# A two-layer transformer trunk on one core: the first key block's value product made 512 queries wide, and the second layer's x turned four blocks earlier

## The chip, the cores and the metric

One core of one Trainium2 chip runs the whole program. The metric is device time in microseconds (us). The kernel before takes 1125.02 us, the median of three runs (1124.52 to 1125.22). One further execution was profiled; every duration below is from that one.

## The reference, cut to what matters

```python
for l in range(2):
    h = rmsnorm(x, attn_norm[l])
    sb_q, sb_k, sb_v, df_q, df_k, df_v = split(h @ w_in[l])          # 1024 -> 6 x 512
    sb_out = stick_breaking_attention(sb_q, sb_k, sb_v)              # 8 heads of 64, weights w, out = w @ v
    df_heads = differential_attention(rope(df_q), rope(df_k), df_v)  # 4 heads, two softmaxes, (p0 - lam*p1) @ v
    df_out = rmsnorm(df_heads, subln_norm[l]) * (1 - lambda_init)
    x = x + concat([sb_out, df_out]) @ w_o[l]
    h = rmsnorm(x, mlp_norm[l])
    x = x + square(relu(h @ w_ff1[l])) @ w_ff2[l]                    # 1024 -> 4096 -> 1024
out = rmsnorm(x, final_norm)
```

There are 512 positions. Query and key blocks are 128 long, and all attention is causal: query block i looks at key blocks 0 to i. Everything is float32.

## The kernel before, in words

**Arithmetic.** A float32 operand is split into a rounded half (`hi`, made by ScalarE) and the rest (`lo`, subtracted on VectorE). A product is three matmuls, hi x hi, hi x lo, lo x hi (`three`, L295), or two where the values are kept as one tile of both halves (the stick-breaking heads, L655 and L656). Weights come from HBM as 512 KB tiles and are split on the chip (`split_part`, L116 on ScalarE and L132 on VectorE), two or four units ahead of TensorE.

**Order of the work.** x lies turned, features on partitions and positions along the free axis. In a layer, TensorE runs a dense stream (input projections `p...`, then the output projection `wo`) and the attention is woven into it: `dense` (L777) yields after every few matmuls, `attn` (L734) is a generator that is advanced as a planner's credit allows (L821 to L846). Attention goes in units: kind (`d` differential, `s` stick-breaking), head block b, m, and half. A unit with half 0 holds query blocks 0 and 1, one with half 1 holds query blocks 2 and 3. A unit passes through three stages, one iteration of L737 apart:

- `s1_df`, `s1_sb` (L547, L569): scores into a PSUM bank of tag `s` (three banks), then the weights on ScalarE, VectorE and GpSimd. Each has two or more score steps.
- `s2` (L621), two iterations later (`LAG2`): transposes of the weights into banks of tag `t` (two of them), then a split into `xh`, `xl` (key blocks 0 and 1) and `zh`, `zl` (key blocks 2 and 3). A half-0 unit writes columns 0 to 383 of `xh` and `xl`: key block 0 for query blocks 0 and 1 in columns 0 to 255, then key block 1 for query block 1. A half-1 unit writes columns 384 to 895, where 640 to 895 are key block 0 for query blocks 2 and 3.
- `s3` (L640), three iterations later (`LAG3`): weights times values into the one bank of tag `o`. The table in L648 to L650 says which columns go where: a half-0 unit multiplies key block 0 for 256 queries, the half-1 unit key block 0 for the other 256, then key block 1 for 384 and key blocks 2 and 3 for 256 each. After that the head's result is read out (L671, L672; L674 splits the last one into `vdh`, `vdl`, which the second half of the output projection reads).

`behind_scores` (L716) sets what follows the score steps of an iteration: for a half-1 unit key blocks 0 and 1, then `s2` of another unit, then key blocks 2 and 3; for a half-0 unit `s2`, then key block 0. `attn` takes one step of this after each score step.

**The dense block behind attention.** The first quarter of the hidden units (group 0) goes in eight blocks f of 24 matmuls each, k = 0 to 7 (L1203). Behind each block stand its evictions (`evict_whole`, L960) and one piece of `h_form` (L998): sums and differences of blocks of h, which the later three groups multiply, seven products instead of eight (`quad_group`, L1034; `FORMS`). Then come the products with the second matrix, in the order `FORMS2` = 11, x3, 21, x2, x1, x4, 22 (L1215), accumulated in chains named X, V, Y, W. Their weights lie in `kept` tiles (names q00 to q20, and the tile `waves` for the sixth). `fetch` (L866) issues the load on SyncE's queue; for form x3 a second load on GpSimd's queue adds another quadrant on top.

**Where the layers differ.** The first layer parks x in HBM and makes the differences of h in x itself. The second layer keeps x, since `forth` (L1113) has to transpose it into the tiles y behind blocks 4 to 7 (L1209 to L1211); its differences are made in three of the `kept` tiles (L981, L982), so the loads into these come late: x3 behind block 6 and 21 behind block 7 (L1019), where the first layer has them behind blocks 3 and 5.

Of the kernel before, what the change touches and what calls it, by code (L numbers as in the profile page):

```python
# [17 lines left out]
P = 128  # L18
# [146 lines left out]
def trunk(ctx, tc, opened, xT, w, w2, w1, gfin, lamv, cos, sin, out):  # L165
# [169 lines left out]
    for l in range(L):  # L335
        with ExitStack() as actx:
# [7 lines left out]
            vd_hi = ap_.tile([P, 4, 512], F32R, tag="vdh", name=f"vdh{l}")  # L344
            vd_lo = ap_.tile([P, 4, 512], F32R, tag="vdl", name=f"vdl{l}")
            ms_hi, ms_lo = vd_hi, vd_lo
            xh, xl = (ap_.tile([P, 896], F32R, tag=f"x{n}", name=f"x{n}{l}") for n in "hl")
            zh, zl = (ap_.tile([P, 512], F32R, tag=f"z{n}", name=f"z{n}{l}") for n in "hl")
            nc.gpsimd.memset(zh[:, 0:128].bitcast(F32), 0.0)
            nc.gpsimd.memset(zl[:, 0:128].bitcast(F32), 0.0)  # L350

            def tt(name):
                return a2.tile([P, S], F32, tag="t", name=name, bufs=TB)
# [284 lines left out]
                yield (0.77 if half else 0.33) + (also() if also else 0.0)  # L638

            def s3(u, parts_):  # L640
                half, b, m, kind = u["half"], u["b"], u["m"], u["kind"]
                key = (kind, b, m)
                if half == 0:
                    heads[key] = bank("o", f"O{l}{kind}{b}{m}")
                k = 2 if kind == "s" else 3
                cost = 0.0
                for kb in parts_:
                    t, at_, to, w = {  # L648
                        (0, 0): ((xh, xl), 0, 0, 256), (1, 0): ((xh, xl), 640, 256, 256), (1, 1): ((xh, xl), 256, 128, 384),
                        (1, 2): ((zh, zl), 256, 256, 256), (1, 3): ((zh, zl), 0, 256, 256)}[(half, kb)]  # L650
                    o = heads[key][:, to : to + w]
                    wh, wl = (e[:, at_ : at_ + w] for e in t)
                    if kind == "s":
                        v = vs[:, kb, 2 * b + m, :]
                        nc.tensor.matmul(o, v, wh, start=(half == 0), stop=False)  # L655
                        nc.tensor.matmul(o, v, wl, start=False, stop=(kb == 3))  # L656
                    else:
                        three(o, (vd_hi[:, kb, b * P : (b + 1) * P], vd_lo[:, kb, b * P : (b + 1) * P]), (wh, wl),
                              half == 0, kb == 3)
                    cost += w * k * MMC  # L660
                if half == 1 and parts_[-1] != 3:
                    yield cost
                    return
                if half == 1:
                    o = heads.pop(key)
                    if kind == "s":
                        if m == 0:
                            heads[("mt", b)] = a2.tile([P, S], F32, tag="mt", name=f"mt{l}{b}", bufs=MTB)
                        mt = heads[("mt", b)]
                        oc = tt(f"oc{l}{b}{m}")[0:64, :]  # L670
                        nc.scalar.copy(oc, o[64:128, :])  # L671
                        nc.vector.tensor_add(mt[64 * m : 64 * m + 64, :], o[0:64, :], oc)  # L672
                        if m == 1:
                            split(ms_hi[:, b, :], ms_lo[:, b, :], mt)  # L674
                    else:
                        os_ = a2.tile([P, S], F32, tag="mt", name=f"os{l}{b}", bufs=MTB)
                        sqo = tt(f"sqo{l}{b}")
                        nc.scalar.activation(sqo, o, AF.Square)
                        nc.scalar.activation(os_, o, AF.Copy, scale=gsub[:, l : l + 1])
                        rc = a3.tile([P, 4], F32, tag="rc", name=f"rc{l}{b}")  # L680
                        late.append((b, os_, sqo, rc))
                yield cost

            units = []
# [43 lines left out]

            def values(u, parts_):
                while not ok(("v" + u["kind"], u["b"])):  # L730
# [119 lines left out]
        with ExitStack() as fctx:  # L850
# [126 lines left out]
                split(hi[:, 6, :], lo[:, 6, :], F[:, 3, :])  # L977

            early, late_ = slice(0, 256), slice(256, 512)
            if last:  # L980
                ta, tb_, tc_ = (kept[k].rearrange("p (a t) -> p a t", a=4) for k in ((1, 0), (1, 1), (2, 0)))  # L981
                td, te = ta, tb_  # L982
            else:
# [14 lines left out]
            def h_form(k):  # L998
                if k == 1:
                    for c in range(4):  # L1000
                        a = nc.scalar.activation(ta[:, c, :], x[:, c, early], AF.Copy, scale=gcol("mlp", l, c))
                        behind(a, ends["h"][0])
                    if last:
                        scaled(tb_, 0, late_, ta, ALU.subtract)
                elif k == 2:
                    scaled(tc_, 4, early, ta, ALU.subtract)
                    if not last:
                        scaled(tb_, 0, late_, ta, ALU.subtract)
                    split(*h_forms["x3"], tb_)
# [9 lines left out]
                for form, at in (("x3", 6 if last else 3), ("21", 7 if last else 5)):  # L1019
                    if k == at:  # L1020
                        for c in range(GP // 2):
                            fetch(0, form, c)

            def temp(k, name):
                if k == 3:
# [353 lines left out]
```

## Time and profile before

| | |
|---|---|
| median of three runs | 1125.02 us |
| the profiled execution: time, span from first to last instruction | 1125.43 us, 1123.7 us |
| TensorE matmul, busy | 1115.3 us (99%) |
| VectorE, ScalarE, GpSimd, busy | 905.5, 683.8, 155.7 us |
| mean granted TensorE clock | 0.999 |
| matmuls | 6421 |

A profile row of a group gives the source line, engine, operation, names (out<-in), shapes and count; a timeline row begins with the start from the span's beginning and the duration, and ends with the idle time before it and who ended it. PE is TensorE's matmul side, PEld its weight loads, DVE is VectorE, ACT ScalarE, POOL GpSimd, SP SyncE; an engine's name with q is its instruction queue. Matmuls are pipelined: the duration of one is longer than the distance between two starts, and only the distance says what one costs.

### The profile page before, as it was taken

The numbers are of one execution on the slowest core, as the hardware profiler recorded it, in microseconds if no ns is written. First come the engines' busy times: TensorE is split into PE (matmuls) and PEld (weight loads), VectorE is DVE, ScalarE is ACT, GpSimd is POOL, SyncE is SP. The second block draws the span as 40 slices with busy tenths as digits, with TensorE's granted clock in tenths as the row PEclk, the third lists the DMA queues.
The fourth block names the chain that finished last, engine by engine and source line by source line (L and its number), as shares of the span: only waits on it lengthen the run. The fifth ranks groups of instructions, "written<-read, shape, count | busy, mean of one in ns | idle before, by whom it ended". The sixth has DMA issues, their size and how long they took to land.

```text
span 1123.7 us, 17281 instructions
## 1 busy us (share of the span) xinstructions
PE 1115.3 (99%) x6421; PEld 979.2 (87%) x6421; DVE 905.5 (81%) x1309; ACT 683.8 (61%) x1107; POOL 155.7 (14%) x233
## 2 busy tenths in 40 slices
PE   9999999999999999999999999999999999999997
PEld 7889889888899899899878898988887998998986
DVE  7788789798668779778877887898877787797787
ACT  6446666667558457467344666665765584674665
POOL 1001344101001001001000014430010110010010
PEclk9999999999999999999999999999999999999999
DMA  7466343268687678748325654522477886687462
GB/s 256 129 190 185 113 135 111 75 226 224 175 213 183 175 192 187 190 131 218 101 75 155 191 146 132 165 61 72 150 193 212 213 188 174 186 185 205 115 131 94
DMA packets 61044, 181.26 MB, mean 161 GB/s; under 512 B 7456, under 2 KB 8736, under 8 KB 60960
## 3 DMA queue, kind: packets, MB, share of 16 engines
q1 hardware_dynamic: 50160, 141.84, 39.6%
q0 software_dynamic: 10368, 37.75, 18.9%
q8 instruction: 51, 0.84, 0.3%
q10 hardware_dynamic: 432, 0.56, 0.1%
q14 instruction: 33, 0.27, 0.1%
HBM read 150.77 MB, written 4.19 MB: 138 GB/s over the span
## 4 chain that ended last, share of the span: by engine, by line
PE 92%; DVE 3%; DMA 2%; issue 1%; ACT 1%; POOL 0%; POOLq 0%; DVEq 0%; ACTq 0%
PE X L299 9%; PE X L301 9%; PE X L300 9%; PE V L299 3%; PE V L301 3%; PE V L300 3%; PE wo L299 3%; PE wo L300 3%; PE wo L301 3%; PE Y L301 2%; PE Y L299 2%; PE Y L300 2%; DMA q<-in_w 2%; DVE wlo L132 1%; PE f L299 1%; PE f L300 1%
## 5 line engine op out<-in xcount | busy, mean ns | idle before, releaser
L116 ACT ACTIVATE whi<-q 128x1024 fp32r<-128x1024 f32 x96 | 101.5, 1059 | 110.9 <-PE X L301 38.3
L132 DVE TENSOR_TENSOR wlo<-q,whi 128x1024 fp32r<-128x1024 f32 x96 | 117.0, 1222 | 50.6 <-ACT whi L116 50.5
L132 DVE TENSOR_TENSOR wlo<-raw,whi 128x1024 fp32r<-128x1024 f32 (+1 forms) x82 | 99.1, 1215 | 9.5 <-ACT whi L116 9.0
L116 ACT ACTIVATE whi<-raw 128x1024 fp32r<-128x1024 f32 (+1 forms) x82 | 80.7, 993 | 33.4 <-issue 9.9
L299 PE MATMUL X<-whi,Ah 128*128 128x512 f32 x248 | 97.7, 394 | 0.2 <-DVE y L1107 0.2
L300 PE MATMUL X<-wlo,Ah 128*128 128x512 f32 x248 | 96.7, 390 | 0.0
L301 PE MATMUL X<-whi,Al 128*128 128x512 f32 x248 | 96.7, 390 | 0.0
L132 DVE TENSOR_TENSOR wlo<-waves,whi 128x1024 fp32r<-128x1024 f32 x40 | 48.9, 1222 | 16.5 <-ACT whi L116 16.4
L116 ACT ACTIVATE whi<-waves 128x1024 fp32r<-128x1024 f32 x40 | 42.2, 1055 | 29.1 <-PE X L301 18.2
L299 PEld LDWEIGHTS X<-whi,Ah 128*128 128x128 f32 x248 | 46.6, 188 | 12.1 <-DVE y L1107 2.0
L301 PEld LDWEIGHTS X<-whi,Al 128*128 128x128 f32 x248 | 46.6, 188 | 9.9
L300 PEld LDWEIGHTS X<-wlo,Ah 128*128 128x128 f32 x248 | 46.6, 188 | 8.9
L301 PE MATMUL X<-h_hi,wlo 128*128 128x256 f32 x192 | 54.3, 283 | 0.0
L299 PE MATMUL X<-hxh,whi 128*128 128x256 f32 x192 | 54.3, 283 | 0.0
L300 PE MATMUL X<-hxl,whi 128*128 128x256 f32 x192 | 54.3, 283 | 0.0
L301 PE MATMUL X<-hxh,wlo 128*128 128x256 f32 x192 | 54.3, 283 | 0.0
L300 PE MATMUL X<-h_lo,whi 128*128 128x256 f32 x192 | 54.3, 283 | 0.0
L299 PE MATMUL X<-h_hi,whi 128*128 128x256 f32 x192 | 54.3, 283 | 0.0
L299 PE MATMUL f<-h_hi,whi 128*128 128x512 f32 x128 | 50.3, 393 | 0.0
L301 PE MATMUL f<-h_hi,wlo 128*128 128x512 f32 x128 | 49.9, 390 | 0.0
L300 PE MATMUL f<-h_lo,whi 128*128 128x512 f32 x128 | 49.8, 389 | 0.0
L239 DVE TENSOR_TENSOR Al<-x,Ah 128x512 fp32r<-128x512 f32 (+1 forms) x60 | 46.6, 793 | 3.8 <-ACT Ah L238 3.5
(748 smaller groups left out, 3726.4 us busy)
## 6 DMA issues: line engine op xcount, KB each, us to landing
raw<-in_w SPq DMA_DIRECT2D x78, 512.0 KB, 3.6
q<-in_w SPq DMA_DIRECT2D x48, 512.0 KB, 4.2
q<-in_w POOLq DMA_DIRECT2D x48, 512.0 KB, 7.8
waves<-in_w SPq DMA_DIRECT2D x28, 512.0 KB, 4.4
first_a<-in_w SPq DMA_DIRECT2D x12, 512.0 KB, 4.6
first_b<-in_w SPq DMA_DIRECT2D x12, 512.0 KB, 5.6
first_c<-in_w SPq DMA_DIRECT2D x12, 512.0 KB, 4.2
first_b<-in_w POOLq DMA_DIRECT2D x12, 512.0 KB, 7.0
```

Source lines behind the costliest of these rows:

```text
L116: return self.nc.scalar.activation(o, src, AF.Copy)
L132: self.last = h, nc.vector.tensor_tensor(out=lo[:, a:b], in0=raw[:, a:b], in1=hi[:, a:b].bitcast(F32), op=ALU.subtract)
L239: nc.vector.tensor_tensor(out=lo, in0=src, in1=hi.bitcast(F32), op=ALU.subtract)
L299: nc.tensor.matmul(pt, ah, bh, start=first, stop=False, skip_group_check=goes_on),
L300: nc.tensor.matmul(pt, ah, bl, start=False, stop=False, skip_group_check=goes_on),
L301: nc.tensor.matmul(pt, al, bh, start=False, stop=last, skip_group_check=goes_on))
```

## The change

**Part one, attention.** `xh`, `xl`, `zh`, `zl` become ranges of one tile `turned_`, so that columns 0 to 255 and 640 to 895 can be read as one operand of 2 x 256 elements (`firsts`). A half-0 unit has no value product any more; the half-1 unit multiplies key block 0 for all 512 queries at once, in one matmul per product, and opens the `o` bank with it. `attn` lets the second score step go ahead of that product (`lead`).

**Part two, second layer.** `forth` runs behind blocks 1 to 4; the pieces of `h_form` stand one block later and write into x as in the first layer; the loads of x3 and 21 are issued behind blocks 3 and 5 in both layers.

```diff
-            xh, xl = (ap_.tile([P, 896], F32R, tag=f"x{n}", name=f"x{n}{l}") for n in "hl")
-            zh, zl = (ap_.tile([P, 512], F32R, tag=f"z{n}", name=f"z{n}{l}") for n in "hl")
+            turned_ = ap_.tile([P, 2816], F32R, tag="turned", name=f"turned{l}")
+            xh, xl, zh, zl = (turned_[:, a:b] for a, b in ((0, 896), (896, 1792), (1792, 2304), (2304, 2816)))
+            firsts = [turned_[:, a : a + 1280].rearrange("p (a t) -> p a t", a=2)[:, :, 0:256] for a in (0, 896)]
...
-                if half == 0:
+                if parts_[0] == 0:
                     heads[key] = bank("o", f"O{l}{kind}{b}{m}")
...
-                    t, at_, to, w = {
-                        (0, 0): ((xh, xl), 0, 0, 256), (1, 0): ((xh, xl), 640, 256, 256), (1, 1): ((xh, xl), 256, 128, 384),
-                        (1, 2): ((zh, zl), 256, 256, 256), (1, 3): ((zh, zl), 0, 256, 256)}[(half, kb)]
...
+                    if kb == 0:
+                        o, w, (wh, wl) = heads[key], S, firsts
+                    else:
+                        t, at_, to, w = {
+                            1: ((xh, xl), 256, 128, 384), 2: ((zh, zl), 256, 256, 256), 3: ((zh, zl), 0, 256, 256)}[kb]
...
-                if u and u["half"] == 1:
+                u = u if u and u["half"] else None
+                if u:
                     yield from values(u, (0, 1))
...
-                    yield from values(u, (2, 3) if u["half"] else (0,))
+                    yield from values(u, (2, 3))
...
+                        lead = i >= LAG3 and units[i - LAG3]["half"]
...
+                            if lead:
+                                lead = 0
+                                continue
...
-            if last:
-                ta, tb_, tc_ = (kept[k].rearrange("p (a t) -> p a t", a=4) for k in ((1, 0), (1, 1), (2, 0)))
-                td, te = ta, tb_
-            else:
-                ta, td = x[:, 0:4, early], x[:, 0:4, late_]
-                tc_, te = x[:, 4:8, early], x[:, 4:8, late_]
-                tb_ = ta
+            ta, td = x[:, 0:4, early], x[:, 0:4, late_]
+            tc_, te = x[:, 4:8, early], x[:, 4:8, late_]
...
-                        h_form(k)
-                        if last and k > 3:
-                            for tb in (2 * (k % 2), 2 * (k % 2) + 1):
-                                forth(tb, 1 - k // 6)
+                        if last and 0 < k < 5:
+                            for tb in (0, 1) if k < 3 else (2, 3):
+                                forth(tb, 1 - k % 2)
+                        h_form(min(k - 1, 5) if last and k < 7 else k)
+                        for form, at in (("x3", 3), ("21", 5)):
+                            if k == at:
+                                for c in range(GP // 2):
+                                    fetch(0, form, c)
```

How this moves instructions is seen at three places. The first is TensorE in the first layer's first differential head (bank `O0d`; `p0s0q` and `p0d3k` are input projections, `S0d` scores). Before, key block 0 stands in two places, with 256 queries each; the first of them:

```order
L301 MATMUL p0d3k<-h_hi,wlo_691 128x512
L299 MATMUL O0d_836<-xh_142,vdh_140 128x256
L300 MATMUL O0d_836<-xl_143,vdh_140 128x256
L301 MATMUL O0d_836<-xh_142,vdl_141 128x256
L299 MATMUL p0d3k<-h_hi,whi_690 128x512
```

and the second, ahead of key block 1:

```order
L299 MATMUL O0d_836<-xh_142,vdh_140 128x256
L300 MATMUL O0d_836<-xl_143,vdh_140 128x256
L301 MATMUL O0d_836<-xh_142,vdl_141 128x256
L299 MATMUL O0d_836<-xh_142,vdh_140 128x384
L300 MATMUL O0d_836<-xl_143,vdh_140 128x384
L301 MATMUL O0d_836<-xh_142,vdl_141 128x384
```

Of the change, the one place that is left:

```order
L546 MATMUL S0d_894<-kl0d2k,st0d2q 128x256
L299 MATMUL p0s0q<-h_hi,whi_781 128x512
L300 MATMUL p0s0q<-h_lo,whi_781 128x512
L301 MATMUL p0s0q<-h_hi,wlo_782 128x512
L299 MATMUL O0d_911<-turned_142,vdh_140 128x512
L300 MATMUL O0d_911<-turned_142,vdh_140 128x512
L301 MATMUL O0d_911<-turned_142,vdl_141 128x512
L299 MATMUL O0d_911<-turned_142,vdh_140 128x384
L300 MATMUL O0d_911<-turned_142,vdh_140 128x384
L301 MATMUL O0d_911<-turned_142,vdl_141 128x384
```

Six matmuls of 256 columns have become three of 512, behind the second score step (`S0d_894`); over the program TensorE has 56 rows fewer.

The second place is SyncE's queue in the second layer, from the last tiles of the first matrix (`raw`) on; `first_a` to `first_c` are weights of group 1, q and `waves` weights of group 0's second products. Before:

```order
L109 DMA raw177_8397<-in_w 128x1024
L900 DMA first_a1_8399<-in_w1 128x1024
L900 DMA first_b1_8405<-in_w1 128x1024
L900 DMA first_c1_8455<-in_w1 128x1024
L868 DMA q10_1_8238<-in_w2 128x1024
L868 DMA q11_1_8239<-in_w2 128x1024
L868 DMA waves_75<-in_w2 128x1024
L868 DMA q20_1_8240<-in_w2 128x1024
```

And of the change:

```order
L109 DMA raw177_8349<-in_w 128x1024
L875 DMA q10_1_8176<-in_w2 128x1024
L875 DMA q11_1_8177<-in_w2 128x1024
L875 DMA q20_1_8178<-in_w2 128x1024
L907 DMA first_a1_8351<-in_w1 128x1024
L907 DMA first_b1_8357<-in_w1 128x1024
L907 DMA first_c1_8429<-in_w1 128x1024
L875 DMA waves_75<-in_w2 128x1024
```

Three loads (q10, q11, q20) have passed the three of group 1; `waves` stays where it was.

The third place is VectorE at the end of the first layer's attention, where the last head (`mt`) is added up and split (`vdl`). Before:

```order
L672 TENSOR_TENSOR mt_2511<-O0s_2535,oc_2553 64x512
L771 TENSOR_TENSOR x<-x,wo_2538 128x512
L132 TENSOR_TENSOR wlo_2567<-raw_2390,whi_2566 128x1024
L239 TENSOR_TENSOR vdl_141<-mt_2511,vdh_140 128x512
L771 TENSOR_TENSOR x<-x,wo_2572 128x512
```

And of the change:

```order
L674 TENSOR_TENSOR mt_2469<-O0s_2499,oc_2511 64x512
L239 TENSOR_TENSOR vdl_141<-mt_2469,vdh_140 128x512
L778 TENSOR_TENSOR x<-x,wo_2520 128x512
L132 TENSOR_TENSOR wlo_2536<-raw_2374,whi_2535 128x1024
L778 TENSOR_TENSOR x<-x,wo_2541 128x512
```

The split of `vdl` has passed an addition to x and a weight split; on ScalarE the rounding of `vdh` has likewise passed that weight's rounding. The second layer has the same exchange.

More of the change, by code (lines that the diff above doesn't have):

```diff
@@ L640, in s3 @@
             def s3(u, parts_):
-                half, b, m, kind = u["half"], u["b"], u["m"], u["kind"]
+                b, m, kind = u["b"], u["m"], u["kind"]
                 key = (kind, b, m)
-                if half == 0:
+                if parts_[0] == 0:
                     heads[key] = bank("o", f"O{l}{kind}{b}{m}")
@@ L647, in s3 @@
                 for kb in parts_:
-                    t, at_, to, w = {
-                        (0, 0): ((xh, xl), 0, 0, 256), (1, 0): ((xh, xl), 640, 256, 256), (1, 1): ((xh, xl), 256, 128, 384),
-                        (1, 2): ((zh, zl), 256, 256, 256), (1, 3): ((zh, zl), 0, 256, 256)}[(half, kb)]
-                    o = heads[key][:, to : to + w]
-                    wh, wl = (e[:, at_ : at_ + w] for e in t)
+                    if kb == 0:
[3 more added lines that the diff above has]
+                            1: ((xh, xl), 256, 128, 384), 2: ((zh, zl), 256, 256, 256), 3: ((zh, zl), 0, 256, 256)}[kb]
+                        o = heads[key][:, to : to + w]
+                        wh, wl = (e[:, at_ : at_ + w] for e in t)
                     if kind == "s":
                         v = vs[:, kb, 2 * b + m, :]
-                        nc.tensor.matmul(o, v, wh, start=(half == 0), stop=False)
+                        nc.tensor.matmul(o, v, wh, start=kb == 0, stop=False)
                         nc.tensor.matmul(o, v, wl, start=False, stop=(kb == 3))
@@ L658, in s3 @@
                         three(o, (vd_hi[:, kb, b * P : (b + 1) * P], vd_lo[:, kb, b * P : (b + 1) * P]), (wh, wl),
-                              half == 0, kb == 3)
+                              kb == 0, kb == 3)
                     cost += w * k * MMC
-                if half == 1 and parts_[-1] != 3:
+                if parts_[-1] != 3:
                     yield cost
                     return
[L664 to L674, printed above, removed]
-                    else:
[L676 to L681, printed above, removed]
@@ new lines, in s3 @@
+                o = heads.pop(key)
+                if kind == "s":
+                    if m == 0:
+                        heads[("mt", b)] = a2.tile([P, S], F32, tag="mt", name=f"mt{l}{b}", bufs=MTB)
+                    mt = heads[("mt", b)]
+                    oc = tt(f"oc{l}{b}{m}")[0:64, :]
+                    nc.scalar.copy(oc, o[64:128, :])
+                    nc.vector.tensor_add(mt[64 * m : 64 * m + 64, :], o[0:64, :], oc)
+                    if m == 1:
+                        split(ms_hi[:, b, :], ms_lo[:, b, :], mt)
+                else:
+                    os_ = a2.tile([P, S], F32, tag="mt", name=f"os{l}{b}", bufs=MTB)
+                    sqo = tt(f"sqo{l}{b}")
+                    nc.scalar.activation(sqo, o, AF.Square)
+                    nc.scalar.activation(os_, o, AF.Copy, scale=gsub[:, l : l + 1])
+                    rc = a3.tile([P, 4], F32, tag="rc", name=f"rc{l}{b}")
+                    late.append((b, os_, sqo, rc))
@@ L979, in trunk @@
             early, late_ = slice(0, 256), slice(256, 512)
-            if last:
-                ta, tb_, tc_ = (kept[k].rearrange("p (a t) -> p a t", a=4) for k in ((1, 0), (1, 1), (2, 0)))
-                td, te = ta, tb_
-            else:
-                ta, td = x[:, 0:4, early], x[:, 0:4, late_]
-                tc_, te = x[:, 4:8, early], x[:, 4:8, late_]
-                tb_ = ta
+            ta, td = x[:, 0:4, early], x[:, 0:4, late_]
+            tc_, te = x[:, 4:8, early], x[:, 4:8, late_]
             h_forms = {"11": [e[:, 0:4, late_] for e in (h_hi, h_lo)], "x4": [e[:, 4:8, early] for e in (h_hi, h_lo)],
@@ L1002, in h_form @@
                         behind(a, ends["h"][0])
-                    if last:
-                        scaled(tb_, 0, late_, ta, ALU.subtract)
                 elif k == 2:
                     scaled(tc_, 4, early, ta, ALU.subtract)
-                    if not last:
-                        scaled(tb_, 0, late_, ta, ALU.subtract)
-                    split(*h_forms["x3"], tb_)
+                    scaled(ta, 0, late_, ta, ALU.subtract)
+                    split(*h_forms["x3"], ta)
                 elif k == 3:
@@ L1018, in h_form @@
                     split(*h_forms["x1"], tc_)
[L1019 to L1022, printed above, removed]
             def temp(k, name):
```

## The prediction

> **What bounds the kernel now.** I read the page first, then the waits of TensorE, then stretches of the two layers against each other, and last the chain of work around the one place where TensorE stands still.
>
> ```profile
> PE 1115.3 (99%) x6421; PEld 979.2 (87%) x6421; DVE 905.5 (81%) x1309; ACT 683.8 (61%) x1107; POOL 155.7 (14%) x233
> PE warm L222 <- POOL edge L216: 1.4, 1, 1.4
> PE Y L300 <- DVE wlo L132: 0.4, 1, 0.4
> PE X L299 <- DVE y L1107: 0.2, 1, 0.2
> ```
>
> TensorE is busy 99% of the span, and the three rows of waits are all that it has: 1.4 us at the start and two short ones. So the time is the sum of the distances between matmul starts. An edit is worth what it takes from that sum, or what it adds as a wait; work on VectorE, ScalarE or the queues counts only when TensorE runs into it.
>
> What one matmul costs is the distance to the next start, not its duration. The first and last rows here are the first layer's dense block, then come the window with two whole `quad_group` calls, and the last head of the first layer's attention:
>
> ```profile
> 269.65 0.39 PE L300 MATMUL f<-h_lo,whi 128*128 128x512 f32 x1
> ...
> 271.01 0.39 PE L300 MATMUL f<-h_lo,whi 128*128 128x512 f32 x1
> 320.61:360.92 40.31, 40.31 (x337) 40.31 (x336) 30.04 (x32) 29.63 (x39) 5.38 (x7) 1.00 0.74 187
> 213.31 0.28 PE L655 MATMUL O0s<-xh,vs 128*128 128x256 f32 x1
> 213.43 0.28 PE L656 MATMUL O0s<-xl,vs 128*128 128x256 f32 x1
> 213.55 0.33 PE L655 MATMUL O0s<-xh,vs 128*128 128x384 f32 x1
> 213.72 0.33 PE L656 MATMUL O0s<-xl,vs 128*128 128x384 f32 x1
> 213.90 0.39 PE L299 MATMUL wo<-mdh,whi 128*128 128x512 f32 x1
> ```
>
> Between the first two are six matmuls of 512 columns: 1.36 us / 6 = 0.227 us. The two calls hold 336 matmuls of 256 columns (7 forms x 2 x 4 x 3, twice), and 40.31 / 336 = 0.120 us. The value products go by the same distances (213.31, 213.43, 213.55). So 256 columns more cost 0.107 us, and about 0.013 us is paid per matmul whatever its width.
>
> **Part one, the value products.** For each of the 4 differential heads three pairs of 256-wide matmuls become three 512-wide ones, for each of the 8 stick-breaking head pairs two pairs: (4 x 3 + 8 x 2) x 2 layers = 56 fewer. Each saves 2 x 0.120 - 0.227 = 0.013 us, so **0.73 us**.
>
> The one thing that the trace does not show is a 512-wide moving operand in two runs of 256. If the second run starts for nothing, it costs 0.227; if each run pays the fixed part, 0.240 and nothing is saved. I take 0.227, the row of the same width, and keep both ends. The far end is the second rival. The price of leaving an operand split, 0.013 us, can also be had from a page: the Trainium skill, TensorE: Matmul & The Clock Gate, section Back-to-back issue gap, gives N/2.4 ns plus 2.5 ns for a warm matmul, by which this term would be an estimated 56 x 2.5 ns = 0.14 us and the kernel 0.6 us slower than I forecast. The rows above disagree with it: they have 13 ns where it has 2.5.
>
> What moves with it: the half-0 unit's product leaves its place and the half-1 unit's goes behind the second score step. Nothing waits longer in front of it, since its operands were split one unit earlier or at the same point as before. The `o` bank is opened later, so it is less of a bottleneck; the second score step comes some 0.8 us earlier, but its bank was last used three score steps before. I cost the moves at nothing. The cover is the dense stream: between a split and its reader stand at least two dense matmuls, and if they were too few, each head would wait for VectorE's 0.5 to 0.7 us.
>
> The tail of each layer's attention has one small gain of its own. These are TensorE and VectorE in the first layer, and TensorE in the second:
>
> ```profile
> 219.16 0.39 PE L301 MATMUL wo<-vdh,wlo 128*128 128x512 f32 x1
> 219.38 0.50 PE L300 MATMUL wo<-vdl,whi 128*128 128x512 f32 x1
> 219.72 0.39 PE L301 MATMUL wo<-vdh,wlo 128*128 128x512 f32 x1
> 218.65 0.68 DVE L239 TENSOR_TENSOR vdl<-mt,vdh 128x512 fp32r<-128x512 f32 x1
> 774.83 0.39 PE L301 MATMUL wo<-vdh,wlo 128*128 128x512 f32 x1
> 775.06 0.50 PE L300 MATMUL wo<-vdl,whi 128*128 128x512 f32 x1
> 775.39 0.40 PE L301 MATMUL wo<-vdh,wlo 128*128 128x512 f32 x1
> ```
>
> The matmul with `vdl` is 0.11 us late in both (0.56 us for two starts instead of 0.454), because VectorE makes `vdl` behind a weight split. The change's order has `vdl` ahead of that split, and TensorE has 23 matmuls (2 + 12 + 9, 5.2 us) between the last head and this reader. **0.2 us** for both layers. The weight split that goes back by one place is for a unit whose turn is 24 matmuls later.
>
> **Part two, the second layer's loads.** The chain of waits from 841 us on, in order of time, and the same stretches of both layers (first layer first; chain Y, 24 matmuls, then from the second X chain's last part on):
>
> ```profile
> 841.61 8.56 DMA q<-in_w
> ...
> 850.25 1.07 ACT whi L116
> ...
> 851.34 1.23 DVE wlo L132
> ...
> 860.74 3.49 DVE wlo L132 x3
> 864.23 0.67 DVE y L1107
> ...
> 864.94 0.50 PE X L299
> 293.22:298.66 5.44, 5.44 (x25) 4.50 (x24) 4.74 (x4) 2.13 (x2) 0.88 (x1) 1.00 0.72 134
> 304.10:309.95 5.85, 5.85 (x26) 4.56 (x25) 2.45 (x2) 3.37 (x5) 0.88 (x1) 1.00 0.55 188
> 852.53:858.71 6.18, 5.75 (x25) 4.38 (x24) 6.15 (x10) 3.41 (x5) 0.00 (x0) 1.00 0.28 85
> 864.15:870.53 6.38, 6.22 (x27) 4.77 (x26) 4.00 (x6) 2.12 (x2) 0.00 (x0) 1.00 1.00 381
> ```
>
> Here the load of q20 (form 21) is issued at 841.61, behind block 7, since q20 held a difference of h until then. It lands 8.56 us later, its split ends at 852.57, and from there VectorE works off what has piled up: DVE is busy 6.15 of 6.18 us while TensorE does chain Y, and 3.49 us of weight splits delay the read-out of X. TensorE loses 6.18 - 5.44 = 0.74 us in chain Y. In the last stretch 26 matmuls take 6.38 us, 0.48 over 26 x 0.227; the first layer's 25 take 5.85, 0.18 over. So 0.30 more: **1.04 us** in all.
>
> The first layer is the model for what comes: its loads stand where the change puts these, and its weights are ready.
>
> ```profile
> 285.62 1.05 ACT L116 ACTIVATE whi<-q 128x1024 fp32r<-128x1024 f32 x1
> 288.88 1.05 ACT L116 ACTIVATE whi<-waves 128x1024 fp32r<-128x1024 f32 x1
> 248.63 1.41 SPq L868 DMA_DIRECT2D q<-in_w  x3
> 800.98 5.64 SPq L109 DMA_DIRECT2D raw<-in_w  x3
> 814.26 0.33 SPq L900 DMA_DIRECT2D first_a<-in_w  x1
> 250.00:260.00 10.00, 10.00 (x46) 8.29 (x45) 10.00 (x21) 7.98 (x13) 1.98 (x2) 1.00 0.92 324
> 808.00:818.00 10.00, 10.00 (x46) 8.29 (x45) 8.90 (x18) 5.99 (x11) 0.00 (x0) 1.00 0.44 140
> 825.34 0.58 ACT L1117 ACTIVATE y<-xT 128x512 f32<-128x512 f32 x1
> ```
>
> There both weights of form 21 are rounded from 285.62 and 288.88 on, before chain Y begins at 293.22. The change issues q10, q11 and q20 behind the raw loads of 800.98, so from about 807 us on, 35 us before q20 now. They pass `first_a` to `first_c`, which group 1 needs only some 50 us later, and GpSimd's two additions for x3 pass the one for `first_b`. The engines have room: 44% busy in 808 to 818, where the first layer ran 92% in its like stretch and TensorE stayed full.
>
> The other moves of part two I cost at nothing. The eight read-outs of the turned x (0.58 us each on ScalarE) come at blocks 1 to 4 instead of 4 to 7, the same 32 transposes behind other blocks; the pieces of `h_form` go one block later with the same 16 VectorE and four ScalarE operations. What covers them is the four-unit lead of the splits and the 5.44 us of a block; if a piece held up a split by more than that lead, TensorE would wait for the rest of it. No reader of the differences comes before group 1.
>
> **The sum.** 0.73 + 0.2 + 1.04 = 1.97 us. The profiled execution took 1125.43 (a span of 1123.7 and 1.7 around it), so 1123.46; the median of the runs lies 0.41 below that execution, so **1123.0**. Its own range is 1122.4 to 1123.7: the 0.73 may be 0, the small terms may be off by a few tenths.
>
> **Rivals.**
>
> - *Part two gives nothing.* VectorE's queue, not the load, would be what delays chain Y: it is busy 6.15 of 6.18 us there. Then only 0.93 goes: 1124.1. Against it: the chain of waits goes back to the load, and the same work in the first layer has VectorE busy 4.74 of 5.44.
> - *The two-run operand streams slowly*, my case for slower than before. The nearest row with a slow stream is the transposes:
>
> ```profile
> 552.55 0.44 PE yT L1124 x4
> ```
>
>   Four transposes of 128 columns take 0.44 us, against 0.227 for 512 columns of a product. If the 56 matmuls ran like that, each would cost 0.44 instead of the pair's 0.240: 56 x 0.20 = 11.2 us lost, less the 1.24 of the other terms, so 1135.0. It decides at 0.262 us per matmul (56 x 0.022 = 1.24), above which the kernel is slower than before. For it: no row shows such a read. Against it: each run has 256 consecutive elements, the width that streams at full rate in the window above.
> - *A new wait of TensorE* in attention or in the second layer's blocks, say one VectorE split (0.7 us) per layer at the tail: 1124.4.
> - *More goes.* In the 256-wide window the weight loads are busy all of the 40.31 us (PEld). If a removed load freed half of what it lasts beyond its matmul, (0.188 - 0.120) / 2 = 0.034 us by the row below, 56 of them would give 1.9 us instead of the 0.73: 1121.8.
>
> ```profile
> L299 PEld LDWEIGHTS X<-whi,Ah 128*128 128x128 f32 x248 | 46.6, 188 | 12.1 <-DVE y L1107 2.0
> ```
>
> **How the numbers follow.** Forecast 0.62; part two gives nothing 0.12; two-run operand slow 0.10, half of it past 0.262 us; a new wait 0.08; more goes 0.08. A measurement of this kernel tells about 0.2% from no change, 2.25 us, so faster means below 1122.8 and slower above 1127.3. Faster holds a third of the forecast and the last rival: 0.28. Slower holds half of the slow operand and a quarter of the new waits: 0.07. The rest, 0.65, is within. The range goes from 1122.1 to 1124.8: it takes in the forecast, part two without effect and the milder waits, and leaves out the slow operand and most of the last rival.
>
> **What would show it.** Right: matmuls of O with 512 columns 0.227 us apart; chain Y of the second layer in 5.44 us with both weights of form 21 rounded before it; no wait of TensorE but the first; 1.97 us less span. Wrong: starts further apart than 0.24 us behind the new matmuls; rows of waits on `turned` or on a block's `whi`, `wlo`; chain Y still longer than 6 us.

## The result, and the profile after

The changed kernel takes 1128.81 us (median of 6 runs, 1128.13 to 1129.13), the kernel before 1124.87 us beside it (6 runs, 1124.45 to 1125.37). The ratio is 1.0034, 95% interval 1.0022 to 1.0047: slower by 3.9 us, where 2.0 us less was forecast. The profiled execution took 1128.86 us, with a span of 1127.1.

The page's row of engines, and all waits of TensorE in the changed kernel (total, times, longest):

```profile
PE 1116.8 (99%) x6365; PEld 977.3 (87%) x6365; DVE 902.5 (80%) x1309; ACT 684.6 (61%) x1107; POOL 149.3 (13%) x233
PE warm L222 <- POOL edge L216: 1.4, 1, 1.4
PE O1s L659 <- DVE turned L239: 0.8, 1, 0.8
PE O0s L659 <- DVE turned L239: 0.8, 1, 0.8
PE S0d L545 <- ACT p0d L602: 0.3, 1, 0.3
PE S1d L545 <- ACT p1d L602: 0.3, 1, 0.3
```

The 56 matmuls are gone (6421 to 6365), yet TensorE is busy for 1.5 us longer. The waits of chain Y have gone; four new rows, the same two in each layer, have come. They hold 2.2 us, about half of the loss; the rest shows only in the distances between starts.

Where in the program? These are TensorE's first transposes of the norm (`rs_a`) and its first dense matmul (`f`) of both layers, so each pair holds one layer's attention. First the changed kernel:

```profile
22.86 0.60 PE L270 MATMUL rs_a<-edge,norms 128*128 128x128 f32 x4
...
240.90 0.39 PE L299 MATMUL f<-h_hi,whi 128*128 128x512 f32 x1
...
581.11 0.66 PE L270 MATMUL rs_a<-edge,norms 128*128 128x128 f32 x4
...
798.44 0.39 PE L299 MATMUL f<-h_hi,whi 128*128 128x512 f32 x1
```

Then the kernel before in a second profile, taken as an experiment below:

```profile
22.53 0.60 PE L270 MATMUL rs_a<-edge,norms 128*128 128x128 f32 x4
...
238.62 0.39 PE L299 MATMUL f<-h_hi,whi 128*128 128x512 f32 x1
...
578.81 0.65 PE L270 MATMUL rs_a<-edge,norms 128*128 128x128 f32 x4
...
794.08 0.39 PE L299 MATMUL f<-h_hi,whi 128*128 128x512 f32 x1
```

Attention takes 218.04 and 217.33 us instead of 216.09 and 215.27: 1.95 + 2.06 = 4.0 us more, the whole loss. Between f and the next `rs_a` both have 340.2 us. I use these two stage lengths for all experiments: they leave out the start, which differs from execution to execution.

**The tail of each layer.** TensorE in the changed kernel, from the transposes of a stick-breaking head's second half to its product; then VectorE in the same stretch:

```profile
204.79 0.93 PE L633 MATMUL T0s<-edge,sig0s 128*128 128x128 f32 x7
...
207.39 0.39 PE L658 MATMUL O0s<-turned,vs 128*128 128x512 f32 x1
208.61 0.50 PE L659 MATMUL O0s<-turned,vs 128*128 128x512 f32 x1 [0.83 <-DVE turned L239]
208.95 0.34 PE L658 MATMUL O0s<-turned,vs 128*128 128x384 f32 x1
```

```profile
202.82 1.39 DVE L132 TENSOR_TENSOR wlo<-raw,whi 128x1024 fp32r<-128x1024 f32 x1
...
204.70 0.68 DVE L674 TENSOR_TENSOR mt<-O0s,oc 64x512 f32<-64x512 f32 x1
205.42 0.96 DVE L563 TENSOR_TENSOR_SCAN C0s<-keep0s,edge 128x384 f32<-128x384 f32 x1
206.29 0.66 DVE L778 TENSOR_TENSOR x<-x,wo 128x512 f32<-128x512 f32 x1
206.87 1.09 DVE L239 TENSOR_TENSOR vdl<-mt,vdh 128x512 fp32r<-128x512 f32 x1
207.88 1.14 DVE L239 TENSOR_TENSOR turned<-T0s,turned 128x512 fp32r<-128x512 f32 x2
```

The same head before, TensorE and VectorE:

```profile
203.79 0.93 PE L632 MATMUL T0s<-edge,sig0s 128*128 128x128 f32 x7
...
206.38 0.28 PE L655 MATMUL O0s<-xh,vs 128*128 128x256 f32 x1
...
207.43 0.28 PE L656 MATMUL O0s<-xl,vs 128*128 128x256 f32 x1
```

```profile
202.88 0.69 DVE L672 TENSOR_TENSOR mt<-O0s,oc 64x512 f32<-64x512 f32 x1 [0.61 <-ACT oc L671]
203.59 0.69 DVE L771 TENSOR_TENSOR x<-x,wo 128x512 f32<-128x512 f32 x1
204.20 0.95 DVE L562 TENSOR_TENSOR_SCAN C0s<-keep0s,edge 128x384 f32<-128x384 f32 x1
205.07 0.67 DVE L239 TENSOR_TENSOR vdl<-mt,vdh 128x512 fp32r<-128x512 f32 x1
205.65 0.68 DVE L239 TENSOR_TENSOR xl<-T0s,xh 128x512 fp32r<-128x512 f32 x1
```

Before, the reader of the `lo` half starts 3.64 us after the transposes (207.43), and the split is done after 2.54 (206.33): 1.1 us to spare. In between stands the half-0 product at 206.38 with the dense step behind it. The change took both out, so the reader's turn comes after 2.83 us (207.62, at 0.23 per matmul). And VectorE is late: the head in front ends later (`mt` starts 0.09 us ahead of the transposes instead of 0.91, since VectorE is on a weight split from 202.82 and then on a split of 0.55 us from 204.12), the addition to x, which came ahead of the scan, now stands behind it, and `vdl` takes 1.09 us instead of 0.67. The first of the two splits begins at 207.88 and, at the 0.68 that it took before, ends 3.8 us after the transposes, 1.2 later than before. TensorE stands from 207.62 to 208.61, 0.99 us, and the next matmul is 0.11 late.

**The second score step of the last differential head.** TensorE and ScalarE in the changed kernel, then TensorE before:

```profile
95.84 0.22 PE L545 MATMUL S0d<-st0d3k,st0d3q 128*128 128x128 f32 x1
...
96.83 0.33 PE L437 MATMUL p0u<-whi,h_hi 128*128 128x256 f32 x1
97.48 0.39 PE L545 MATMUL S0d<-st0d3k,st0d3q 128*128 128x256 f32 x1 [0.31 <-ACT p0d L602]
```

```profile
95.70 1.06 ACT L116 ACTIVATE whi<-raw 128x1024 fp32r<-128x1024 f32 x1
96.67 0.67 ACT L602 ACTIVATE p0d<-S0d,sm0d 128x512 f32<-128x512 f32 x1
```

```profile
95.36 0.22 PE L544 MATMUL S0d<-st0d3k,st0d3q 128*128 128x128 f32 x1
...
96.51 0.28 PE L299 MATMUL O0d<-xh,vdh 128*128 128x256 f32 x1
...
99.54 0.28 PE L544 MATMUL S0d<-st0d3k,st0d3q 128*128 128x256 f32 x1
```

Before, the head's second score step came 4.2 us after its first: the value product of key blocks 0 and 1 (from 96.51 to 97.39) and 2.15 us of dense matmuls stood in between. Now it is asked for 1.1 us after it (96.83 + 0.12). Its bank is the one of three score steps ago, and ScalarE reads that from 96.67 to 97.34, behind a weight's rounding. TensorE loses 97.48 - 96.95 = 0.53 us.

By the distances between starts one layer has: 0.99 + 0.11 at the tail, 0.53 + 0.10 here, 0.27 + 0.10 at the first stick-breaking head (115.6), and 0.25 in a row of transposes at 195.3: 2.35 us. Less 0.11 for `vdl`, which no longer comes late, and 28 x 0.009 = 0.25 for the wider matmuls: 1.99, where the stages show 1.95 and 2.06. The second layer has the same seven late starts to within 0.01 us; smaller ones of 0.06 to 0.22 us, in both kernels, are left out of this sum.

### The profile page after: what moved, and what is told of

It reads as the page before. It is cut to its first block, busy times and chain, and to the rows that moved or that the text cites. A ratio compares the mean times of both kernels' runs of the same rounds, so it can differ in the third digit from the quotient of the medians.

```text
span 1127.1 us, 17174 instructions
## 1 busy us (share of the span) xinstructions
PE 1116.8 (99%) x6365; PEld 977.3 (87%) x6365; DVE 902.5 (80%) x1309; ACT 684.6 (61%) x1107; POOL 149.3 (13%) x233
## 4 chain that ended last, share of the span: by engine, by line
PE 95%; DVE 3%; issue 1%; ACT 1%; POOL 0%; POOLq 0%; DVEq 0%
PE X L299 9%; PE X L300 9%; PE X L301 9%; PE V L299 4%; PE V L300 4%; PE V L301 4%; PE f L301 3%; PE f L299 3%; PE f L300 3%; PE wo L299 2%; PE wo L301 2%; PE wo L300 2%; PE Y L300 2%; PE Y L301 2%; PE Y L299 2%; PE W L300 1%
## 5 line engine op out<-in xcount | busy, mean ns | idle before, releaser
L132 DVE TENSOR_TENSOR wlo<-raw,whi 128x1024 fp32r<-128x1024 f32 (+1 forms) x82 | 95.9, 1175 | 8.5 <-ACT whi L116 7.4
```

The source lines that it names most:

```text
L132: self.last = h, nc.vector.tensor_tensor(out=lo[:, a:b], in0=raw[:, a:b], in1=hi[:, a:b].bitcast(F32), op=ALU.subtract)
```

## The experiments

**Theory.** The product that was removed and the dense step behind it were the distance between a split and its reader; the `lead` took a like distance from between two score steps. The loss is waits. **Rivals:** the two-run operand streams slowly; one tile makes readers wait for the wrong writers; part two costs something.

| kernel | us (median) | before beside it | attention 1 | attention 2 | chain Y |
|---|---|---|---|---|---|
| before, first profile | 1125.02 | | 216.18 | 215.42 | 6.19 |
| before again | 1125.31 | 1125.14 | 216.09 | 215.27 | 5.44 |
| changed | 1128.81 | 1124.87 | 218.04 | 217.33 | 5.44 |
| part two alone | 1125.02 | 1125.00 | 216.15 | 215.27 | 5.44 |
| part one alone | 1128.52 | 1125.00 | 218.01 | 217.29 | 5.44 |
| one tile | 1124.93 | 1125.14 | 216.15 | 215.73 | 5.44 |
| two matmuls at the new place | 1129.10 | 1125.00 | 218.22 | 217.65 | 5.44 |
| no lead | 1126.03 | 1125.00 | 216.78 | 216.08 | 5.44 |
| two steps at the tail | 1126.72 | 1125.14 | 217.05 | 216.35 | 5.44 |
| lead late | 1127.63 | 1125.36 | 217.47 | 216.75 | 5.44 |
| lead late, steps at the tail | 1126.77 | 1125.36 | 217.05 | 216.44 | 5.44 |
| no lead, one step ahead | 1124.78 | 1125.14 | 216.07 | 215.40 | 5.44 |
| no lead, two steps ahead | 1128.90 | 1125.36 | 217.98 | 217.49 | 5.44 |
| step in place | 1124.56 | 1125.10 | 215.98 | 215.35 | 5.44 |

**Part two alone**: the diff's hunks from `early, late_` on, attention as before.

> Part two without part one. Theory (part one's new waits of TensorE cost all of the loss, part two works as foretold): 1.0 us less than before, 1123.9. Rival (part two gives nothing, or costs something elsewhere, and the loss is spread over both parts): 1124.9 or more.

1125.02 against 1125.00, ratio 0.9998 (0.9990 to 1.0007). Part two brings nothing, as the rival had it, though its own profile shows chain Y in 5.44 us.

**Part one alone**: the other hunks.

> Part one without part two. Theory: the whole loss and 1.0 us more, since part two's gain is missing: 1129.8, with the waits at the tail (0.99 us for the second matmul of a stick-breaking head) and at the scores (0.53 and 0.27 us) in both layers as in the changed kernel. Rival (part two costs): below 1128.8.

1128.52, ratio 1.0033 (1.0020 to 1.0045), with the four rows of waits. The whole loss is part one's. The median lies 0.3 us on the rival's side of 1128.8, far inside the interval, and part two alone cost nothing. The 1.0 us more did not come: chain Y takes 5.44 us here too, with the late loads of before.

**The kernel before, again**, for the question that these two raise.

> The kernel before, unchanged, for a second profile of it. Part two alone has brought nothing, though its profile shows chain Y in 5.44 us. Theory (the 1.04 us of waits round chain Y in the first profile belonged to that execution, made up for there by a start that was 0.7 us shorter than in the other profiles): chain Y of the second layer in under 5.7 us here, the start before 20 us some 0.7 us longer, the time as before. Rival (the wait is there each time, and part two loses as much at another place): chain Y in 6.2 us again.

1125.31, ratio 1.0 (0.9991 to 1.001). TensorE's one wait is that of the start, and chain Y takes 5.44 us. The stretch of chain Y here and in the changed kernel, and the load of q20 (form 21) here:

```profile
852.60:858.04 5.44, 5.44 (x25) 4.50 (x24) 5.41 (x7) 2.61 (x3) 0.00 (x0) 1.00 0.28 96
```

```profile
856.98:862.42 5.44, 5.44 (x26) 4.51 (x24) 4.73 (x4) 2.13 (x2) 0.86 (x1) 1.00 0.67 138
```

```profile
840.80 0.33 SPq L868 DMA_DIRECT2D q<-in_w  x1
```

VectorE is as full as the first profile had it (5.41 of 5.44), and TensorE loses nothing. The load starts at 840.80, 0.8 us ahead of the first product of X (841.62); in the first profile the two came together (841.61 and 841.55), and there TensorE ran into it. The load goes out when the split of h that reads its tile ends (841.59 there, 840.78 here). In part one alone it starts 0.4 us ahead of X (845.65 and 846.04), again without a wait. That these tenths decide it is my reading; what made that split late in the first profile is not shown. Of four profiles with the old order of loads (before twice, part one alone, one tile) one has the wait. The theory holds: the 1.04 us belonged to one execution. The start was shorter in that one, by 0.4 us against this profile (`rs_a` at 22.15 and 22.53) and by 0.7 against the changed kernel's, so that its 1125.43 lies within the spread of the runs here (up to 1125.83).

**One tile**: the tile line alone.

```diff
-            xh, xl = (ap_.tile([P, 896], F32R, tag=f"x{n}", name=f"x{n}{l}") for n in "hl")
-            zh, zl = (ap_.tile([P, 512], F32R, tag=f"z{n}", name=f"z{n}{l}") for n in "hl")
+            turned_ = ap_.tile([P, 2816], F32R, tag="turned", name=f"turned{l}")
+            xh, xl, zh, zl = (turned_[:, a:b] for a, b in ((0, 896), (896, 1792), (1792, 2304), (2304, 2816)))
```

> The kernel before, with xh, xl, zh and zl as ranges of one tile and nothing else: every engine has the order of before. Theory: no change, 1125.0, no wait on turned. Rival (one tile makes readers of one range wait for writers of another): rows of waits on turned and 1 to 4 us more. It is also a third profile of the order of before: by the theory that chain Y's wait comes in some executions only, its chain Y takes anything from 5.44 to 6.2 us.

1124.93, ratio 0.9997 (0.9988 to 1.0006), no wait on `turned`. The rival falls. (The 0.4 us more in its second attention is one wait for a transfer of keys, at 652 us.)

**Two matmuls at the new place.**

```diff
+                    runs = [(o, wh, wl)] if kb else [
+                        (o[:, 256 * r : 256 * r + 256], wh[:, r, :], wl[:, r, :]) for r in range(2)]
+                    for r, (o, wh, wl) in enumerate(runs):
...
```

> The changed kernel, but key block 0's product is two matmuls of 256 columns again, back to back at the new place: 56 matmuls more, nothing else moved. Theory (a two-run operand streams at 0.231 us, the pair at 0.240): 56 x 0.009 = 0.5 us more, 1129.3, and the waits stay. Rival (the two-run operand is what costs): the time falls back below 1126.

1129.10, ratio 1.0038 (1.0025 to 1.0050), with the same four rows of waits, each within 0.15 us of the changed kernel's, and one more at the start (0.5 us for a weight's rounding, at 6.1 us). Attention is 0.18 + 0.32 = 0.50 us longer than in the changed kernel, which is 56 x 0.009; as the waits differ too, it is good to some tenths. The same product in the changed kernel, and here:

```profile
200.05 0.40 PE L658 MATMUL O0s<-turned,vs 128*128 128x512 f32 x1
200.28 0.39 PE L659 MATMUL O0s<-turned,vs 128*128 128x512 f32 x1
200.51 0.33 PE L658 MATMUL O0s<-turned,vs 128*128 128x384 f32 x1
```

```profile
200.96 0.28 PE L661 MATMUL O0s<-turned,vs 128*128 128x256 f32 x1
...
201.44 0.34 PE L661 MATMUL O0s<-turned,vs 128*128 128x384 f32 x1
```

0.46 us for two matmuls of 512 columns, against 0.48 for four of 256. The two-run operand is not slow: the rival falls. The Trainium skill, TensorE: Matmul & The Clock Gate, section Back-to-back issue gap, has 2.5 ns per matmul beyond the columns, by which this would be an estimated 0.14 us; the stages show 0.50.

**No lead.**

```diff
-                        lead = i >= LAG3 and units[i - LAG3]["half"]
+                        lead = 0
```

> The changed kernel, but the second score step no longer goes ahead of the value product. Theory (a score step that comes earlier runs into a bank of scores that is still being read): the waits of S0d and S0s (0.53 and 0.27 us per layer, with 0.2 us of slow starts behind them) go, 2 us in all, 1126.8; but the product now follows its split one score step and one dense step earlier, about 1 us, so waits on the split of turned may come at the heads of the dense part: each of up to 0.5 us, 12 heads a layer, so up to 1130 or more. The wait at the tail stays, since no score step stands there. Rival (the lead is what keeps the products from waiting and the scores are free): slower than 1128.8.

1126.03, ratio 1.0009 (1.0000 to 1.0018). The waits at the scores go, as expected; waits on `turned` come at only one more head per layer (155.6, 0.47 us), far from the twelve that I allowed for, and the tail's halves to 0.47. The stages are 1.26 + 1.25 = 2.5 us shorter than in the changed kernel, the time 2.8: the lead is the larger part of the loss.

**Two steps at the tail.** A `yield 0` lets one dense step of three matmuls go first.

```diff
                 if u:
+                    for _ in range(2 * (i == n)):
+                        yield 0
                     yield from values(u, (0, 1))
```

> The changed kernel with two dense steps (6 matmuls, 1.36 us) ahead of the value product that waits at each layer's tail. Theory: the 0.99 us and the 0.11 behind it go in both layers, 2.2 us in all, 1126.6; the waits at the scores stay. Rival (VectorE is simply late there and the wait turns up at the next reader): 1128 or more, with the wait at the next head or at vdl.

1126.72, ratio 1.0012 (1.0003 to 1.0021), no wait on `turned`: 0.99 and 0.98 us less in the two layers, a little under the theory's 1.1 each; with 2.1 us less in the time, the tail is half of the loss.

**Lead late**, and **lead late with steps at the tail**.

```diff
-                        lead = i >= LAG3 and units[i - LAG3]["half"]
+                        lead = i >= 10 and units[i - LAG3]["half"]
```

> The changed kernel, but the lead only from iteration 10 on: at the three heads before (iterations 4, 6 and 8) the product stands ahead of the second score step again. Theory (the score step that goes ahead meets a bank that ScalarE has not read yet): the waits of S0d and S0s go in both layers, 0.53 + 0.27 + 0.2 us of slow starts each, 2.0 us in all: 1126.8; the tail keeps its wait. Rival (those waits only move to the product, which now stands closer behind its split, or to the next score step): above 1128.

1127.63, ratio 1.0020 (1.0012 to 1.0029): 0.57 and 0.58 us less per layer, not 1.0. The waits of S0d and S0s at 97 and 116 us go. The tail's wait, which was to stay, goes too: the two matmuls of that product start at 206.68 and 206.92. But the list has a new row of waits for each layer, 0.7 us for T0s and for T1s. The first layer's, on TensorE and VectorE:

```profile
194.00 0.60 PE L633 MATMUL T0s<-edge,sig0s 128*128 128x128 f32 x4
195.27 0.55 PE L633 MATMUL T0s<-edge,sig0s 128*128 128x128 f32 x3 [0.67 <-DVE turned L239]
```

```profile
193.35 1.39 DVE L132 TENSOR_TENSOR wlo<-raw,whi 128x1024 fp32r<-128x1024 f32 x1
194.67 0.54 DVE L239 TENSOR_TENSOR turned<-T0s,turned 128x384 fp32r<-128x384 f32 x1
```

The transposes of one head wait until the split has read the last head's bank, and that split waits behind a weight split. Only the three heads before were edited, so it is the pace of what follows that has shifted. The place is not new: it is the row of transposes that loses 0.25 us at 195.3 in the changed kernel, behind the same two splits. Smaller late starts have come besides, at 129.4 (0.22 us) and 212.2 us (0.26).

With the two dense steps at the tail besides:

> The lead from iteration 10 on, and two dense steps ahead of the waiting product of the tail: each wait mended at its place, the rest of the change kept. Theory (the loss is these two waits, and they add): 1128.8 - 2.0 - 2.1 = 1124.7. Rival (there is a third loss, in the two-run operand or elsewhere): 1126 or more.

1126.77, ratio 1.0013 (1.0005 to 1.0022), not 1124.7, and not under the tail steps alone (1126.72): the wait of T0s is there again, and the steps at the tail found little left to remove (0.42 and 0.31 us less in the stages than lead late). That the waits add and can be mended one by one is wrong. Nor does this speak for a third loss in the operand: T0s takes 0.87 us in each layer by the distances between starts, most of the 0.96 and 1.17 us that the stages have over before.

**No lead, one step ahead of each product, and two.** Of the diff, the line that differs from no lead:

```diff
                 if u:
+                    yield 0
                     yield from values(u, (0, 1))
```

> The changed kernel without the lead, and with one dense step (0.69 us) ahead of each product of key blocks 0 and 1, about what the two removed places held. Theory (the product needs the distance from its split that the half-0 product and its dense step gave): no wait of TensorE on turned or on the scores; 1126.0 less the two waits of 0.58 us per layer that are left without the lead, so 1123.7 or somewhat above. Rival (the distance is not what counts, or the later products push new waits to the end of each layer): 1126 or more.

1124.78, ratio 0.9997 (0.9988 to 1.0005). No row of waits but the start; attention is back at 216.07 and 215.40, with one late start of 0.27 us left in each layer, at a product at 160 us. Of the loss of 4.0 us in the stages, leaving out the lead takes back 2.5 and the dense step 1.4: without the lead, distance is what was missing. The step with the lead kept was not run, so the two shares hold for this order only.

> No lead, and two dense steps instead of one ahead of each product of key blocks 0 and 1. Theory: the one wait that one step left (0.27 us and the slow start behind it, in both layers) goes, so 0.6 us less than with one step: 1124.2. Rival (more dense work spent there is missing at the end of the layer, where the last head's split has to be covered): a new wait at vdl, 1124.8 or more.

1128.90, ratio 1.0032 (1.0019 to 1.0044): the rival's side, and far beyond its 1124.8, though not at `vdl`. The late start at 160 us goes, but attention falls behind: the last head's transposes stand at 219.5 us, among the second half of the output projection, and wait for their weights (`sig0s`, from GpSimd), in the second layer too; and `wo` waits once in each layer for the values that VectorE splits (the first at 178.0 us):

```profile
PE T0s L633 <- POOL sig0s L566: 1.0, 1, 1.0
PE wo L299 <- DVE vs L420: 0.5, 2, 0.3
```

**Step in place.** No lead (its line as above), and the dense step where the half-0 product stood:

```diff
+                first_half = u and not u["half"]
                 u = u if u and u["half"] else None
...
                 if u:
                     yield from values(u, (2, 3))
+                elif first_half:
+                    yield 0
```

> No lead, and one dense step at the very place where the half-0 product stood: the order of before with that product taken out and its place held by dense work. Theory (what the removed product gave was distance between a split and its reader; held at its place, the wide product saves its 0.5 us and waits nowhere): no wait of TensorE, 0.3 to 0.5 us under the variant with the step ahead of the product, 1124.3. Rival (holding the place upsets the pace elsewhere, as the mending of single places did): a wait at another place, 1125 or more.

1124.56 against 1125.10, ratio 0.9996 (0.9987 to 1.0005), and no row of waits but the start. The loss of the change is gone, and with part two in it this is the lowest median of all; it cannot be told from the kernel before. It is 0.2 us under the step ahead of the product, where the theory had 0.3 to 0.5. Attention is 0.11 us shorter and 0.08 longer than in the second profile of before (0.20 and 0.07 shorter than in the first), not 0.25 shorter in each: part of the wide product's saving goes into a start at the last head that is still late, 0.27 us in each layer:

```profile
215.16 0.40 PE L301 MATMUL wo<-vdh,wlo 128*128 128x512 f32 x1
215.66 0.50 PE L658 MATMUL O0s<-turned,vs 128*128 128x512 f32 x1
```

## Why the prediction was wrong, point by point

- *Fewer matmuls, 0.73 us.* Right in kind. The wide product goes at 0.227 to 0.233 us, so a pair saves 0.009 and not 0.013, and the term is 0.50. The range given for the two-run read held it, and the rival of the slow stream is refuted.
- *The moves of part one, nothing.* **This step failed.** The prediction said: "Nothing waits longer in front of it, since its operands were split one unit earlier or at the same point as before", and took for cover "at least two dense matmuls". I looked at when an operand is split and not at when its reader comes: with the half-0 product went 0.24 us and the dense step behind it, and the reader came 0.8 us nearer to the transposes than before, while VectorE got there 1.2 us later. The spare 1.1 us could be read in the trace of before. Together these are the wait of 0.99 us at each tail, which two dense steps there took away; without the lead, one dense step per head was worth 1.4 us in the stages.
- *The second score step, "some 0.8 us earlier".* The same step, second half: at the last differential head it was 3 us (4.2 to 1.1 us behind the first), since the whole product and 2.15 us of dense matmuls no longer stood in between, and "three score steps before" said nothing about when ScalarE reads that bank. This is the larger half: leaving out the lead took 2.5 of the 4.0 us off the stages, through its own waits at the scores (1.0 us per layer) and through the pace of what follows.
- *The rival of a new wait* named the tail and the right engine, at 0.7 us per layer. The four places make 2.35 us per layer, and it had a chance of 0.08.
- *`vdl`, 0.2 us.* Right: the late start of 0.11 us at each tail is gone.
- *Part two, 1.04 us.* The wait was read rightly in that profile, but its size was that of one execution. The change leaves VectorE busy for 4.73 of the 5.44 us, so that it would remove the wait is likely; with the wait in one of four profiles of the old order, it is not shown. The rival "part two gives nothing" came true for another reason than the one given: VectorE's queue does not delay chain Y by itself, as 5.41 of 5.44 us busy without a wait shows.

With what was measured the sum is 4.70 for the waits, less 0.50, 0.2 and nothing for part two: 4.0 us more. Against the 1124.87 beside it that is 1128.9, where 1128.81 was measured. What stays open is why just these heads wait and not others: I take it to be the pace of the planner, which each edit moved, but no run isolates it.

## What to carry to other kernels

Work that is taken out of a full engine was also distance between a producer and its reader: measure the spare time of every reader that moves (here 1.1 us between split and product) before you price a move at nothing, and put other work in the place that is vacated. A wait that is to be removed should be looked for in a second profile, since one execution can hold a wait of 1 us that the next does not have. Where a planner paces two streams, mending a wait at one place can move others: the lead from iteration 10 on took three waits away and made a fourth larger, and two gains did not add.

## What was unexpected in the hardware

At the start TensorE runs at half its rate, and for how long differs between executions. These are consecutive matmuls of 512 columns in the first profile of before, and in that of the changed kernel:

```profile
5.04 0.39 PE L783 MATMUL p<-h_hi,wlo 128*128 128x512 f32 x1
5.27 0.43 PE L783 MATMUL p<-h_hi,whi 128*128 128x512 f32 x1
```

```profile
5.34 0.63 PE L790 MATMUL p<-h_hi,wlo 128*128 128x512 f32 x1
5.77 0.63 PE L790 MATMUL p<-h_hi,whi 128*128 128x512 f32 x1
```

0.23 and 0.43 us apart, while the windows show a granted clock of 1.00 for both. Over the profiles `rs_a` starts between 22.15 and 23.46 us, and single runs of one kernel spread by about 1 us and more. Not all of this is the slow rate: the latest of these starts holds the wait of 0.5 us for a weight that is told above, and how much of the spread of the runs comes from the start is not shown. The Trainium skill, TensorE: Matmul & The Clock Gate, section What's actually happening, has a cold array at half the rate until a free-running window has been busy, so that the number of slow matmuls differs from run to run; the trace agrees, with matmuls 0.43 us apart where 0.23 is the later distance, and more of them in one execution than in the other.
